# Fewer and larger parts of a down projection, its last weights kept, and a fixed place for some sums

## The chip, the cores and the metric

The kernel runs on one core of a Trainium2 chip. The metric is the device time of one execution in microseconds (us). TensorE (PE) multiplies matrices, VectorE (DVE) and ScalarE (ACT) work on rows of data, GpSimd (POOL) helps in a few places, and the queue of SyncE (SP) issues nearly all transfers between the on-chip memory and DRAM. TensorE accumulates into banks of PSUM; everything else lives in the on-chip memory, 128 partitions wide.

## The reference, cut to what matters

The reference is one layer of a decoder. 1024 prompt rows and 8 rows of running samples go through three branches, whose results are merged and projected; then comes a norm, a gated feed-forward block and a second norm.

```python
    h = layer_norm(ALPHA * x + merged @ w_out, ln1_g, ln1_b)
    gt, up = jnp.split(h @ w_gate_up, 2, axis=-1)
    h = layer_norm(ALPHA * h + (jax.nn.silu(gt) * up) @ w_down, ln2_g, ln2_b)
```

The model width is 1024 and the feed-forward width is 2816, that is 22 tiles of 128 features. All is float32.

## The kernel before, in words

Activations are kept with the features on the partitions and the 1032 rows (1024 + 8) as columns. A float32 product is made of three products of a shorter type: each operand is split into a high half (a cast on ScalarE, line 77) and a low half (what is left, a subtraction on VectorE, line 78), and high x high, high x low and low x high are accumulated in one PSUM bank (`mm3`, lines 116 to 118). So each weight piece that comes from DRAM costs one load, one cast and one subtraction before TensorE can use it.

The end of the kernel, where the change lies, has these stages:

- The output projection (`out_proj`) goes over four quarters of 258 columns. When a quarter's sums are complete, its norm (`quarter_norm`) is made while TensorE works on the next quarter: mean, differences, squares, variance, reciprocal root, product, gain and bias, store of h to DRAM, and the split of h into halves hh and hl. The norm of the last quarter runs beside the next stage.
- The first two feature tiles of gate and up (`plain_gate_up`) are plain products of h, quarter by quarter (tiles fg and fu, then ft and G). The fourth quarter of them needs the halves of the last quarter of h. Between the quarters, steps of `h_combos` are written: sums and differences of quarters of h (tile ht, and R in place, lines 1119 to 1127) with their splits (hth, htl).
- The other twenty feature tiles (`gate_up`) use those sums in a fast scheme with seven products instead of eight. Each finished tile G is stored to DRAM (line 1327).
- The down projection (`down`) reads the 22 tiles back in parts of 6, 6, 6 and 4 into two pools, gA and gB, in turn (tiles gl, the casts gh). A part is multiplied for each of 8 output tiles and three column chunks of 384, 390 and 258 columns, with its own piece of the weights (tiles wd), and added to the accumulators acc (line 1221). The accumulators start as h read back and scaled (lines 1210 and 1211).
- The last part goes chunk by chunk over all outputs (tiles dl, weights wdl), so that a chunk's second norm (`layer_norm`) can run beside the products of the next chunk. The weights of this part are loaded and split again in each of the three chunks. The third chunk has its own norm, `last_layer_norm`: it corrects the sums with the mean of the first two output tiles (tiles c0h, c0l, c and the matrix shift), and sums columns with the matrix ones (tile le) at the very end. Its scaled rows are stored, which ends the kernel.

In these stages the program order isn't the order of the queues: a planner places each instruction on its engine by estimated costs, as soon as what it needs is estimated to be ready, and an engine then executes its queue in that order. Two things bind it: data, and `issue_after(ins)`, which puts the instructions of a block, as far as they are on the engine of `ins`, behind `ins` in that engine's queue. The parts of a norm are written with it behind the last matmul of a product (`norm_step`). Pools lie on a left and a right stack of the on-chip memory; with `reuse_waits="tile"` a new tile waits for the old tiles that overlap it and not for the whole old pool. gA and gB lie on the right, where the halves of h (pool tq) and their sums (pool tx) were.

Of the kernel before, what the change touches and what calls it, by code (L numbers as in the profile page):

```python
# [10 lines left out]
F32 = mybir.dt.float32  # L11
# [7 lines left out]
P = 128  # L19
# [8 lines left out]
NM = 256  # L28
NF = 22
DEC_AT = (1, 2, 4)  # L30
FPARTS = ((0, 6), (6, 6), (12, 6), (18, 4))
PLAIN = 2
GS = 1040
NORM_AT = (0, 3)
# [25 lines left out]
class Builder:  # L60
# [14 lines left out]
    def split(self, hi, lo, src):  # L75

        ins = self.nc.scalar.copy(hi, src).ins  # L77
        self.nc.vector.tensor_sub(lo, src, hi.bitcast(F32))  # L78
        return ins

    def behind(self, ins, other):
# [886 lines left out]
    def last_layer_norm(self, n, r, product, gcol, emit):  # L968


        nc, ph = self.nc, self.ph
        ones = self.ones.bitcast(F32)
        tile_ = lambda tag, name, bufs, dt=F32: ph.tile([P, WIDE], dt, tag=tag, name=name, bufs=bufs)[:, :n]
        s1, s2 = tile_("s1", "ls1", 1), tile_("s2", "ls2", 1)
        hi, lo = (ph.tile([P, n], F32R, tag=f"c0{e}", name=f"c0{e}", bufs=1) for e in "hl")
        e1, e2 = self.bank("t", "le1")[:, :n], self.bank("t", "le2")[:, :n]

        def account(m):
            sq = s2 if m == 0 else tile_("sq", f"lsq{m}", 2)
            nc.scalar.activation(sq, r[m], AF.Square)  # L980
            if m == 7:
                return sq
            if m == 1:
                nc.vector.tensor_add(s1, r[0], r[1])
            elif m:
                nc.vector.tensor_add(s1, s1, r[m])
            if m:
                nc.gpsimd.tensor_add(s2, s2, sq)

        for m in range(KT):  # L990
            ps = product(m, last=m < LATE)
            if m in NORM_AT:
                self.norm_step()
            if m >= LATE:
                nc.tensor.matmul(ps, self.shift, hi, start=False, stop=False)
                nc.tensor.matmul(ps, self.shift, lo, start=False, stop=True)
            nc.vector.scalar_tensor_tensor(r[m], ps, 0.5, r[m], op0=ALU.mult, op1=ALU.add)
            if m == 1:
                s = tile_("xres", "lc0", 3)
                nc.vector.tensor_add(s, r[0], r[1])  # L1000
                self.split(hi, lo, s)
            elif m == LATE - 1:
                with self.tc.issue_after(self.last_mm):
                    c0 = self.bank("o", "c0")[:, :n]
                    nc.tensor.matmul(c0, self.shift, hi, start=True, stop=False)
                    nc.tensor.matmul(c0, self.shift, lo, start=False, stop=True)
                for k in range(LATE):
                    nc.vector.scalar_tensor_tensor(r[k], c0, 0.5, r[k], op0=ALU.mult, op1=ALU.add)
                    account(k)
            elif m >= LATE:  # L1010
                sq = account(m)
        nc.tensor.matmul(e1, ones, s1, start=True, stop=False)
        nc.tensor.matmul(e2, ones, s2, start=True, stop=False)
        nc.tensor.matmul(e1, ones, r[7], start=False, stop=True)
        nc.tensor.matmul(e2, ones, sq, start=False, stop=True)
        mu, rs = tile_("xres", "lmu", 3), tile_("gt", "lrs", 3)
        nc.scalar.activation(rs, e1, AF.Square)
        nc.scalar.copy(mu, e1)
        nc.vector.tensor_sub(rs, e2, rs)
        nc.scalar.activation(rs, rs, AF.Sqrt, bias=self.vec[:, V_EPS:V_EPS + 1])  # L1020
        for m in range(KT):
            (nc.vector if m < 3 else nc.gpsimd).tensor_sub(r[m], r[m], mu)
        nc.vector.reciprocal(rs, rs)
        self.norm_step()
# [8 lines left out]
    def quarter_norm(self, q, s1, h):  # L1033

        nc, r, vec = self.nc, self.R, self.vec
        cast = lambda a: a.unsqueeze(1).to_broadcast([P, 4, QN])
        yield
        mu = self.col_mean(s1, QN, f"n1mu{q}")
        sq = []
        for kh in range(2):  # L1040
            nc.vector.tensor_sub(r[q, kh], r[q, kh], cast(mu))
            sq.append(self.tq.tile([P, 4, QN], F32, tag=f"q{q}{kh}", name=f"sq{q}{kh}", bufs=2))
            nc.scalar.activation(sq[kh], r[q, kh], AF.Square)
        nc.vector.tensor_add(sq[0], sq[0], sq[1])
        nc.vector.tensor_add(sq[0][:, 0:2, :], sq[0][:, 0:2, :], sq[0][:, 2:4, :])
        nc.vector.tensor_add(sq[0][:, 0, :], sq[0][:, 0, :], sq[0][:, 1, :])
        yield
        var = self.col_mean(sq[0][:, 0, :], QN, f"n1va{q}")
        rs = self.ph.tile([P, QN], F32, tag="rs", name=f"n1rs{q}", bufs=1)
        nc.scalar.activation(rs, var, AF.Sqrt, bias=vec[:, V_EPS:V_EPS + 1])  # L1050
        nc.vector.reciprocal(rs, rs)
        for kh in range(2):
            nc.vector.tensor_mul(r[q, kh], r[q, kh], cast(rs))
            h[q, kh] = self.quarter_pair(q, kh, "h")
            for k in range(4):
                m = 4 * kh + k
                v = r[q, kh][:, k, :]
                nc.scalar.activation(v, v, AF.Identity, bias=vec[:, V_B1 + m:V_B1 + m + 1],
                                     scale=vec[:, V_G1 + m:V_G1 + m + 1])
            nc.sync.dma_start(self.scr["h"][:, 4 * kh:4 * kh + 4, q * QN:(q + 1) * QN], r[q, kh])  # L1060
            self.split(*h[q, kh], r[q, kh])

    def out_proj(self, merged):
        nc, io, ph = self.nc, self.io, self.ph
# [66 lines left out]
    def plain_gate_up(self, f, h, steps):  # L1131

        nc, io = self.nc, self.io
        wg = self.weights(io["wgu"][f], D, f"wfg{f}")
        wu = self.weights(io["wgu"][NF + f], D, f"wfu{f}")
        out = self.zt(f"G{f}")
        for q in range(4):
            x = [tuple(a[:, k % 4, :] for a in h[q, k // 4]) for k in range(KT)]
            pg = self.bank(("s", "t")[q % 2], f"fg{f}_{q}")[:, :QN]
            self.mm3(pg, list(zip(wg, x)))  # L1140
            self.norm_step()
            t = self.ph.tile([P, QN], F32, tag="gt", name=f"ft{f}_{q}", bufs=3)
            nc.scalar.activation(t, pg, AF.Tanh, scale=0.5)
            nc.vector.scalar_tensor_tensor(t, t, 1.0, pg, op0=ALU.add, op1=ALU.mult)
            pu = self.bank("mm", f"fu{f}_{q}")[:, :QN]
            self.mm3(pu, list(zip(wu, x)))
            nc.vector.tensor_mul(out[:, q * QN:(q + 1) * QN], t, pu)
            if f or q:
                next(steps, None)
        nc.sync.dma_start(self.scr["f"][:, f, :], out)  # L1150

    def plain(self, h):
# [34 lines left out]
        for _ in copies:  # L1187
            pass

    def down(self, pools):  # L1190

        nc, io, ph = self.nc, self.io, self.ph

        def load(part):
            f0, nf = FPARTS[part]
            out = []
            for j in range(nf):
                hi, lo = (pools[part % 2].tile([P, GS], F32R, tag=f"g{e}", name=f"g{e}{f0 + j}", bufs=6) for e in "hl")
                nc.sync.dma_start(lo[:, :T].bitcast(F32), self.scr["f"][:, f0 + j, :])
                out.append([(hi[:, t0:t0 + n], lo[:, t0:t0 + n]) for t0, n in CH])  # L1200
            for c in range(3):
# [2 lines left out]
                    self.split(hi, lo, lo.bitcast(F32))  # L1204
            return out

        acc = [self.zt(f"acc{m}") for m in range(KT)]
        gs = [load(0)]
        for m in range(KT):
            nc.sync.dma_start(acc[m], self.scr["h"][:, m, :])  # L1210
            nc.scalar.mul(acc[m], acc[m], ALPHA)
        for part in range(3):
            f0, nf = FPARTS[part]
            gs.append(load(part + 1))
            g = gs[part]
# [6 lines left out]
        self.norm = None  # L1222
        f0, nf = FPARTS[3]
        for c, (t0, n) in enumerate(CH):
            rs = [acc[m][:, t0:t0 + n] for m in range(KT)]

            def product(m, last=True, c=c, n=n):
                w = self.weights(io["wdn"][m][:, f0 * P:(f0 + nf) * P], nf * P, f"wdl{m}_{c}")
                ps = self.bank(("mm", "s")[m % 2], f"dl{m}_{c}")[:, :n]
                self.mm3(ps, [(w[k], gs[3][k][c]) for k in range(nf)], last)  # L1230
                return ps

            def emit(m, v, scale=1.0, t0=t0, n=n):
# [18 lines left out]
    def build(self):  # L1252
# [15 lines left out]
        with ExitStack() as right:  # L1268
# [26 lines left out]
            with pool("zf") as self.z:  # L1295
# [10 lines left out]
                with pool("gA", "right") as ga, pool("gB", "right") as gb, pool("ph5") as self.ph:  # L1306
                    self.lw = WIDE
                    self.down((ga, gb))


class FinishGate:
# [163 lines left out]
```

## Time and profile before

| what | value |
|---|---|
| median of 3 runs | 1996.84 us (1995.01 to 1997.18) |
| the profiled execution's own time | 1994.09 us |
| its span, first to last instruction | 1992.3 us |
| mean granted TensorE clock | 0.989 |
| TensorE busy | 97% |
| VectorE, ScalarE, GpSimd busy | 68%, 49%, 5% |
| fast feature tiles, 1292 to 1694 us | TensorE 402.0 of 402 us busy |
| down products up to the last part, 1694 to 1905 us | TensorE 207.6 of 211 us busy |
| last part up to the closing sums, 1905 to 1976 us | TensorE 55.6 of 71 us busy |
| from there to the end, 1976 to 1992.3 us | TensorE 2.9 of 16.3 us busy |

Times in the profile count from the first instruction. A line of the timeline has the start, the duration, the engine with its source line and operation, the tile written and the tiles read, and in brackets how long the engine stood idle before and what ended it. A line of the waits has who waited for whom, the sum in us, how often, and the longest. Matmuls overlap in the records, so the pace is taken from how many start in a stretch. An "x8" means that many instructions merged into a line.

### The profile page before, as it was taken

How to read it: one execution, taken by the hardware profiler on the slowest of the kernel's cores; microseconds unless marked ns; L12 is line 12 of the kernel's file. 1: busy time of each engine (PE TensorE's matmuls, PEld its weight loads, DVE VectorE, ACT ScalarE, POOL GpSimd, SP SyncE). 2: the span in 40 equal slices, each digit the busy share in tenths (PEclk: the TensorE clock that was granted, in tenths of full speed). 3: DMA queues.
4: the chain of work that ended last, by engine and by line, in shares of the span. 5: the costliest groups of instructions: out<-in, count | busy, mean ns of one | idle time of the engine just before them, and what ended most of it. 6: DMA issues, size and time to landing. Idle time of an engine off the chain costs nothing.

```text
span 1992.3 us, 37520 instructions
## 1 busy us (share of the span) xinstructions
PE 1934.4 (97%) x14524; PEld 1899.4 (95%) x14524; DVE 1350.9 (68%) x2746; ACT 982.8 (49%) x2099; POOL 96.7 (5%) x152
## 2 busy tenths in 40 slices
PE   9999999999999999999999999999999999999994
PEld 9999999999999998988899999899999999999994
DVE  7878987886866565498777567766565655543378
ACT  6555565464666445397764254434333333522134
POOL 1000010010000000021210000000000000000001
PEclk9999999999999999999999999999999999999997
DMA  8554545455323377667334251232222222632122
GB/s 316 168 164 160 175 163 187 136 190 172 135 91 120 124 260 236 167 190 211 109 101 157 75 199 44 71 102 92 93 87 100 86 86 80 247 112 90 58 80 101
DMA packets 155699, 275.67 MB, mean 138 GB/s; under 512 B 18992, under 2 KB 73344, under 8 KB 155520
## 3 DMA queue, kind: packets, MB, share of 16 engines
q1 hardware_dynamic: 154752, 271.17, 42.0%
q8 instruction: 114, 1.87, 0.4%
q0 software_dynamic: 768, 2.10, 0.3%
q14 instruction: 65, 0.53, 0.1%
HBM read 204.19 MB, written 73.18 MB: 139 GB/s over the span
## 4 chain that ended last, share of the span: by engine, by line
PE 82%; DMA 6%; DVE 5%; ACT 5%; issue 2%; SPq 0%; ACTq 0%; DVEq 0%; POOL 0%; POOLq 0%
PE ub L243 5%; PE ub L241 5%; PE ub L242 5%; PE ubf L241 4%; PE ubf L242 4%; PE ubf L243 4%; PE d L116 3%; PE d L117 3%; PE d L118 3%; PE ud L243 2%; PE ud L242 2%; PE ud L241 2%; PE udf L241 2%; PE udf L242 2%; PE udf L243 2%
## 5 line engine op out<-in xcount | busy, mean ns | idle before, releaser
L116 PE MATMUL d<-gh,wd_h 128*128 128x258 f32 (+2 forms) x432 | 138.3, 322 | 3.1 <-ACT gh L77 2.1
L117 PE MATMUL d<-gl,wd_h 128*128 128x390 f32 (+2 forms) x432 | 138.9, 322 | 0.2 <-DVE gl L78 0.2
L118 PE MATMUL d<-gh,wd_l 128*128 128x390 f32 (+2 forms) x432 | 138.6, 322 | 0.0
L1221 DVE SCALAR_TENSOR_TENSOR acc<-d,acc 128x384 f32<-128x384 f32 (+2 forms) x72 | 36.9, 515 | 94.3 <-PE d L118 91.5
L116 PEld LDWEIGHTS d<-gh,wd_h 128*128 128x128 f32 x432 | 81.4, 189 | 4.4 <-ACT gh L77 3.0
L117 PEld LDWEIGHTS d<-gl,wd_h 128*128 128x128 f32 x432 | 81.7, 189 | 0.5 <-DVE gl L78 0.4
L118 PEld LDWEIGHTS d<-gh,wd_l 128*128 128x128 f32 x432 | 82.0, 190 | 0.0
L118 PE MATMUL op<-mh,wol 128*128 128x258 f32 x256 | 72.3, 282 | 1.3 <-DVE wol L78 1.3
L116 PE MATMUL op<-mh,woh 128*128 128x258 f32 x256 | 72.5, 283 | 0.0
L117 PE MATMUL op<-ml,woh 128*128 128x258 f32 x256 | 72.1, 282 | 0.0
L241 PE MATMUL ub<-th,u_4h 128*128 128x258 f32 x240 | 68.6, 286 | 3.3 <-ACT u2s L266 3.3
L594 ACT ACTIVATE bp<-bp,bst 128x257 f32<-128x257 f32 (+1 forms) x128 | 62.8, 493 | 17.3 <-DVE bst L590 17.0
L241 PE MATMUL ub<-th,u_0h 128*128 128x258 f32 x240 | 68.3, 284 | 1.1 <-ACT zb L1346 1.1
L243 PE MATMUL ub<-th,u_4l 128*128 128x258 f32 x240 | 68.9, 287 | 0.0
L242 PE MATMUL ub<-tl,u_4h 128*128 128x258 f32 x240 | 68.4, 285 | 0.0
L241 PE MATMUL ub<-th,u_2h 128*128 128x258 f32 x240 | 68.0, 283 | 0.3 <-ACT p1s L266 0.3
L243 PE MATMUL uc<-th,u_3l 128*128 128x258 f32 x240 | 68.2, 284 | 0.0
L243 PE MATMUL ub<-th,u_2l 128*128 128x258 f32 x240 | 68.2, 284 | 0.0
L243 PE MATMUL ud<-th,u_1l 128*128 128x258 f32 x240 | 68.2, 284 | 0.0
L243 PE MATMUL ub<-th,u_0l 128*128 128x258 f32 x240 | 68.2, 284 | 0.0
L243 PE MATMUL ub<-th,u_6l 128*128 128x258 f32 x240 | 68.2, 284 | 0.0
L243 PE MATMUL ud<-th,u_5l 128*128 128x258 f32 x240 | 68.1, 284 | 0.0
(880 smaller groups left out, 7879.0 us busy)
## 6 DMA issues: line engine op xcount, KB each, us to landing
ur<-win SPq DMA_DIRECT2D x120, 256.0 KB, 2.9
urf<-wgu SPq DMA_DIRECT2D x80, 256.0 KB, 2.7
scr_f<-G SPq DMA_DIRECT2D x22, 516.0 KB, 2.8
gl<-scr_f SPq DMA_DIRECT2D x22, 516.0 KB, 5.9
dck<-cmk SPq DMA_DIRECT2D x32, 256.0 KB, 3.0
dcv<-cmvT SPq DMA_DIRECT2D x32, 256.0 KB, 3.5
st<-scr_q SPq DMA_DIRECT2D x32, 256.0 KB, 4.6
scr_g<-za SPq DMA_DIRECT2D x12, 516.0 KB, 3.4
```

The costliest lines, as they stand in the source:

```text
L116: nc.tensor.matmul(ps, sh, mh, start=opens and i == 0, stop=False)
L117: nc.tensor.matmul(ps, sh, ml, start=False, stop=False)
L118: self.last_mm = nc.tensor.matmul(ps, sl, mh, start=False, stop=closes and i == last).ins
L241: mm(sh[:, w], xh, start=opens and k == 0, stop=False)
L242: mm(sh[:, w], xl, start=False, stop=False)
L243: self.last_mm = mm(sl[:, w], xh, start=False, stop=k == 3).ins
L594: nc.scalar.activation(x, x, AF.Exp, bias=st[:, g:g + 1], scale=-1.0, accum_out=st[:, 4 + g:5 + g])
L1221: nc.vector.scalar_tensor_tensor(a, ps, 0.5, a, op0=ALU.mult, op1=ALU.add)
```

## The change

The down projection has three parts of 8, 7 and 7 feature tiles. The first and third use pool gA (8 buffers of each half), the second gB (7). Only two parts are accumulated over all outputs; the third is the last part. After the second part pool gB is closed and a pool wl takes its place; it holds the split weights of the last part for all eight outputs (16 tiles of 896 columns), which are loaded and split in the first chunk, in pieces of 512 and 384 columns, and used again in the second and third. Three small tiles of the last norm get fewer buffers. In `plain_gate_up`, the steps of `h_combos` are put behind `norm_end`, the last subtraction of the last quarter's norm, in VectorE's queue.

```diff
-FPARTS = ((0, 6), (6, 6), (12, 6), (18, 4))
+FPARTS = ((0, 8), (8, 7), (15, 7))
...
         ins = self.nc.scalar.copy(hi, src).ins
-        self.nc.vector.tensor_sub(lo, src, hi.bitcast(F32))
+        self.last_lo = self.nc.vector.tensor_sub(lo, src, hi.bitcast(F32)).ins
         return ins
...
-                s = tile_("xres", "lc0", 3)
+                s = tile_("xres", "lc0", 2)
...
-        mu, rs = tile_("xres", "lmu", 3), tile_("gt", "lrs", 3)
+        mu, rs = tile_("xres", "lmu", 2), tile_("gt", "lrs", 1)
...
             self.split(*h[q, kh], r[q, kh])
+        self.norm_end = self.last_lo
...
             if f or q:
-                next(steps, None)
+                with self.tc.issue_after(self.norm_end):
+                    next(steps, None)
...
-    def down(self, pools):
+    def down(self, ga, pool):
...
-        def load(part):
+        def load(part, pool):
             f0, nf = FPARTS[part]
-            out = []
+            out, bufs = [], FPARTS[part % 2][1]
             for j in range(nf):
-                hi, lo = (pools[part % 2].tile([P, GS], F32R, tag=f"g{e}", name=f"g{e}{f0 + j}", bufs=6) for e in "hl")
+                hi, lo = (pool.tile([P, GS], F32R, tag=f"g{e}", name=f"g{e}{f0 + j}", bufs=bufs) for e in "hl")
...
+        acc = [self.zt(f"acc{m}") for m in range(KT)]
+        with pool("gB", "right") as gb:
+            g0 = load(0, ga)
+            for m in range(KT):
+                nc.sync.dma_start(acc[m], self.scr["h"][:, m, :])
+                nc.scalar.mul(acc[m], acc[m], ALPHA)
+            g1 = load(1, gb)
+            product(0, g0)
+            g2 = load(2, ga)
+            product(1, g1)
+        with pool("wl", "right") as wl:
+            self.last_products(acc, g2, wl)
+
+    def last_products(self, acc, g, pool):
+        nc, io, ph = self.nc, self.io, self.ph
+        self.norm, w = None, []
+        f0, nf = FPARTS[2]
         for c, (t0, n) in enumerate(CH):
             rs = [acc[m][:, t0:t0 + n] for m in range(KT)]

             def product(m, last=True, c=c, n=n):
-                w = self.weights(io["wdn"][m][:, f0 * P:(f0 + nf) * P], nf * P, f"wdl{m}_{c}")
+                if c == 0:
+                    hi, lo = (pool.tile([P, nf * P], F32R, tag="wl", name=f"wl{e}{m}", bufs=16) for e in "hl")
+                    for a, b in ((0, 512), (512, nf * P)):
+                        raw = self.half_raw(io["wdn"][m][:, f0 * P + a:f0 * P + b], b - a, f"wl{m}r{a}")
+                        self.split(hi[:, a:b], lo[:, a:b], raw[:, :b - a])
+                    w.append([(hi[:, k * P:(k + 1) * P], lo[:, k * P:(k + 1) * P]) for k in range(nf)])
                 ps = self.bank(("mm", "s")[m % 2], f"dl{m}_{c}")[:, :n]
-                self.mm3(ps, [(w[k], gs[3][k][c]) for k in range(nf)], last)
+                self.mm3(ps, [(w[m][k], g[k][c]) for k in range(nf)], last)
                 return ps
```

More of the change, by code (lines that the diff above doesn't have):

```diff
@@ L1205, in load, with product @@
             return out
[L1207 to L1212, printed above, removed]
+        def product(part, g):
             f0, nf = FPARTS[part]
-            gs.append(load(part + 1))
-            g = gs[part]
             for m in range(KT):
@@ L1221, in down @@
                     nc.vector.scalar_tensor_tensor(a, ps, 0.5, a, op0=ALU.mult, op1=ALU.add)
-        self.norm = None
-        f0, nf = FPARTS[3]
+        acc = [self.zt(f"acc{m}") for m in range(KT)]
[14 more added lines that the diff above has]
+        f0, nf = FPARTS[2]
         for c, (t0, n) in enumerate(CH):
@@ L1305, in build @@
                 right.close()
-                with pool("gA", "right") as ga, pool("gB", "right") as gb, pool("ph5") as self.ph:
+                with pool("gA", "right") as ga, pool("ph5") as self.ph:
                     self.lw = WIDE
-                    self.down((ga, gb))
+                    self.down(ga, pool)
 class FinishGate:
```

## The prediction

> **What bounds the kernel now.** I read the sums of the page first, then busy time by stage, then TensorE's waits, then VectorE's order of work where those waits fall.
>
> ```profile
> PE 1934.4 (97%) x14524; PEld 1899.4 (95%) x14524; DVE 1350.9 (68%) x2746; ACT 982.8 (49%) x2099; POOL 96.7 (5%) x152
> ...
> 1300.00:1400.00 100.00, 100.00 (x834) 100.00 (x833) 60.27 (x95) 38.88 (x79) 0.00 (x0) 1.00 0.28 94
> 1800.00:1900.00 100.00, 100.00 (x637) 100.00 (x636) 35.22 (x72) 17.50 (x36) 0.00 (x0) 1.00 0.24 73
> ...
> 1253.00:1268.00 15.00, 10.66 (x64) 9.65 (x63) 10.80 (x13) 9.05 (x15) 0.00 (x0) 0.77 0.32 105
> ...
> 1905.00:1976.00 71.00, 55.56 (x310) 52.77 (x309) 62.00 (x118) 32.07 (x61) 5.04 (x6) 0.90 0.28 82
> 1976.00:1992.30 16.30, 2.85 (x8) 1.76 (x8) 10.72 (x21) 9.53 (x20) 3.63 (x5) 0.52 0.46 163
> ```
>
> TensorE is the bound nearly everywhere, so a change that keeps the number of matmuls can only win where TensorE stands or runs at a lower clock. The full pace is 100/834 = 0.120 us for a matmul of 258 columns and, over the mix of 384, 390 and 258 columns in the down products, 100/637 = 0.157 us, or 0.47 us for one set of three. (In these rows the second field of each engine is its count; the field after POOL is the granted clock.)
>
> Two stretches fall short. Between 1253 and 1268 us only 64 matmuls ran: 64 x 0.120 = 7.7 us of work in 15, so 7.3 us are lost, at a granted clock of 0.77. The last quarter of the output projection's norm falls there. Between 1905 and 1976 us the last part of the down products runs: 4 tiles x 8 outputs x 3 terms = 96 sets at 0.47 = 45.1 us, and some 2.7 us of small matmuls for the norms (eighteen, which I put at 0.15 each by the paces above), so 47.8 of 71 us: 23.2 us are lost.
>
> ```profile
> PE dl L118 <- DVE wdl_l L78: 8.4, 3, 5.3
> PE le L1012 <- DVE ls L986: 2.6, 1, 2.6
> PE fg L116 <- DVE ft L1144: 2.5, 1, 2.5
> PE d L116 <- ACT gh L77: 2.1, 2, 1.3
> PE fg L116 <- ACT hh L77: 1.4, 1, 1.4
> ...
> 1941.32 4.31 DVE L955 SCALAR_TENSOR_TENSOR acc<-acc,vec,n2rs 128x384 f32<-128x384 f32 x8
> 1946.50 0.68 DVE L78 TENSOR_TENSOR wdl_l<-wdl_1r__24009,wdl_h 128x512 fp32r<-128x512 f32 x1
> ...
> 1942.00:1946.00 4.00, 0.00 (x0) 0.00 (x0) 4.00 (x8) 4.00 (x8) 0.00 (x0) 1.00 0.65 234
> 1946.00:1950.00 4.00, 2.77 (x8) 2.77 (x9) 3.46 (x7) 0.28 (x1) 0.00 (x0) 0.51 0.81 235
> ```
>
> The longest wait of the tail is for the low half of reloaded weights (8.4 us). The split of one piece takes 0.68 us, but in VectorE's queue it stands behind eight scalings of the norm of chunk 0 (4.31 us): TensorE does nothing from 1942 to 1946 and then runs at a clock of 0.51.
>
> **The change part by part.** First, the sums of h. Now the sums and splits for the fast units stand between the links of the last quarter's norm:
>
> ```profile
> 1242.10 1.23 DVE L1119 TENSOR_TENSOR ht<-R,R 128x1032 f32<-128x1032 f32 x1
> 1243.25 1.22 DVE L1044 TENSOR_TENSOR sq<-sq,sq 128x1032 f32<-128x1032 f32 x1
> 1244.39 1.23 DVE L1122 TENSOR_TENSOR R<-R,R 128x1032 f32<-128x1032 f32 x1
> 1245.53 0.69 DVE L1045 TENSOR_TENSOR sq<-sq 128x516 f32<-128x516 f32 x1
> ...
> 1249.77 1.22 DVE L78 TENSOR_TENSOR htl<-R,hth 128x1032 fp32r<-128x1032 f32 x1
> 1250.92 1.76 DVE L1051 RECIPROCAL n1rs<-n1rs 128x258 f32<-128x258 f32 x1
> 1252.59 1.17 DVE L89 SCALAR_TENSOR_TENSOR htl<-R,hth 128x1032 fp32r<-128x1032 f32 x1
> 1253.68 2.36 DVE L1053 TENSOR_TENSOR R<-R,n1rs 128x1032 f32<-128x1032 f32 x2
> ...
> 1258.48 1.23 DVE L78 TENSOR_TENSOR hl<-R,hh 128x1032 fp32r<-128x1032 f32 x1 [0.63 <-ACT hh L77]
> ...
> 1262.06 1.23 DVE L78 TENSOR_TENSOR hl<-R,hh 128x1032 fp32r<-128x1032 f32 x1
> 1263.21 0.68 DVE L78 TENSOR_TENSOR wfg_l<-wfg1r__16461,wfg_h 128x512 fp32r<-128x512 f32 x1
> ...
> 1248.97 0.48 ACT L1050 ACTIVATE n1rs<-n1va3p,vec 128x258 f32<-128x258 f32 x1 [0.28 <-PE n1va3p L930]
> ```
>
> L1122 delays L1045 by 1.14 us, two more keep the reciprocal back from 1249.45, where the square root ended, to 1250.92 (1.47), and L89 delays L1053 by 1.09: 3.7 us for certain. L1119 ahead of L1044, and a split ahead of the variance's low half, add up to 1.15 us each. I take 5 of 3.7 to 6.0. The halves hl then come at 1253.5 and 1257.1 instead of 1258.5 and 1262.1 and are done 1.2 us later. TensorE, out of work at about 1253.5, waits some 1.2 us for the first, has 24 matmuls (2.9 us) on it, and some 0.7 us for the second: 1.9 us. What is late next: the moved operations, eight of about 1.15 us for the first half of the columns, now start together at about 1258, and beside them stand four splits of the second feature tile's weights (0.68 us each), needed from about 1261. If all four go behind all eight, TensorE waits until 1258.3 + 9.2 + 0.7 = 1268, 7 us; if they slip between, nothing. The fast units themselves want the sums only near 1290. I take 1.4 us, since the splits depend on nothing but a free buffer and each moved operation depends on one before it: 7.3 - 1.9 - 1.4 = **4.0 us won** (between 5.4 won and 1.6 lost).
>
> A clock of 0.77 over these 15 us is 3.4 us of clock, so 2 to 3 of the 7.3 us come from the clock and not from waiting. I take it as whole once the waits are short; if it is halved all the same, 4.0 becomes about 2. [...]
>
> Second, the drains. Three parts instead of four take 24 accumulations off VectorE; they lie beside a busy TensorE (VectorE 35% between 1800 and 1900, TensorE 100%). Won: 0. Without that cover nothing would be lost, since the work only shrinks.
>
> Third, the opening of the down products. Part 0 grows from 6 to 8 feature tiles:
>
> ```profile
> gl<-scr_f SPq DMA_DIRECT2D x22, 516.0 KB, 5.9
> ...
> 1689.64 2.16 SPq L1199 DMA_DIRECT2D gl<-scr_f  x4
> 1696.35 0.32 SPq L1327 DMA_DIRECT2D scr_f<-G  x1
> 1696.72 1.32 SPq L1199 DMA_DIRECT2D gl<-scr_f  x2
> 1698.09 5.09 SPq L1210 DMA_DIRECT2D acc<-scr_h  x8
> ...
> 1704.00:1712.00 8.00, 6.30 (x35) 5.82 (x36) 4.97 (x11) 7.48 (x13) 0.00 (x0) 1.00 1.03 416
> ```
>
> The queue of SP has four loads, then waits for the last gate product's store, then two loads. The DMA engines are full (share 1.03, 416 GB/s), so a load of 516 KB (0.53 MB) costs 1.27 us, two more 2.5 us, and the loads of acc behind them are that much later. The two tiles that now come after the store give TensorE 2 x 3 x 0.47 = 2.8 us of work on the first output, which covers the 2.5 if four loads still go ahead of the store. If all eight go behind it, the last lands about 4 x 1.27 + 2.5 = 7.6 us later than now's last. I take **1 us lost**, between 1 won and 6 lost (7.6, less part of that cover).
>
> Fourth, the kept weights go into the space of part 1's feature tiles. Each product of part 1 reads them all, so the first kept piece can be written only while the last group of 21 matmuls (2.5 us) runs. Cast and split (0.62 and 0.68 us for 512 columns) fit under it if they wait tile by tile; if they wait for the whole space, TensorE stands about 1.5 us. I take **0.5 us lost**, between 0 and 1.5. Afterwards an output has 1.1 + 1.2 us of casts and splits beside 21 matmuls of 384 columns, some 3.6 us: covered.
>
> Fifth, the tail. Chunks 1 and 2 no longer reload: 16 loads, 16 casts and 16 splits (16 x 0.68 = 10.9 us of VectorE) fall away there, and with 7 tiles instead of 4 the matmuls over the same norms grow by 7/4. The last part is now 168 sets, 79.0 us, with the 2.7 us of small ones. VectorE's work in chunk 2, beside 168 x 0.120 = 20.2 us and about 2 us of small matmuls:
>
> ```profile
> L946 DVE TENSOR_TENSOR n2s<-n2s,n2sq 128x384 f32<-128x384 f32 (+1 forms) x14 | 7.8, 556 | 0.1
> L953 DVE RECIPROCAL n2rs<-n2rs 128x384 f32<-128x384 f32 (+1 forms) x2 | 5.1, 2562 | 0.0
> L942 DVE TENSOR_TENSOR acc<-acc,n2mu1p 128x390 f32<-128x390 f32 x8 | 4.2, 556 | 0.0
> L997 DVE SCALAR_TENSOR_TENSOR acc<-dl,acc 128x258 f32<-128x258 f32 x8 | 3.3, 420 | 0.7 <-PE dl L118 0.5 <-PE dl L996 0.2
> ...
> 1968.36 5.44 POOL L988 TENSOR_TENSOR ls<-ls,lsq 128x258 f32<-128x258 f32 x6 [937.91 <-ACT lsq L980]
> 1970.29 1.22 DVE L78 TENSOR_TENSOR wdl_l<-wdl_2r__24265,wdl_h 128x512 fp32r<-128x512 f32 x1
> ```
>
> Half of L946 (3.9), L942 (4.2), L997 (3.3), four splits of sums (2), twelve corrections and sums of 0.4 (5) make 18.4 us; the reciprocal (2.6) and eight scalings (4.3) come to 25.3. The first 18.4 fit under 22; the rest may be put after the last product, as half of the scalings is now. The variance of chunk 1, 12 us of chained work after its mean, is ready at about 13 of those 22 us, the shift's correction at 15, GpSimd's six additions (5.4) at about 21.5, so that almost nothing is left to wait for. Remaining waits: 1.0 for the variance and the correction, whose places in TensorE's order are fixed beforehand, 1.5 for a reciprocal (2.6) put among the last sums, 0.3 for the two means: 2.8. So 23.2 - 2.8 = **20.4 us won** (22.5 if two thirds of the waits vanish, 12 if VectorE, slowed beside GpSimd as the split of 1.22 us was, becomes the bound). After the last product I take 0: up to 2 us may be won if more scalings come before it.
>
> Sum: 4.0 - 1 - 0.5 + 20.4 = 22.9 us. The profiled execution took 1994.09 us (span 1992.3), so it would be 1971.2; the median of the runs shown lies 2.75 above it, which I keep: 1996.84 - 22.9 = **1973.9**.
>
> **Rivals.** (a) The sums' wait passes to the weights of the second feature tile: 1.6 lost instead of 4.0 won, 1979.5. For it: both queue on VectorE at 1258; against it: the present order is mixed one by one. (b) The opening waits: all eight loads behind the store, 6 instead of 1 lost, 1978.9. For it: two already are. (c) The tail becomes VectorE's: 12 instead of 20.4 won, 1982.3. For it: 62 of 71 us busy now; against it: 10.9 us leave. (d) Slower: part 0's eight loads go behind the store and share the DMA engines evenly with the eight of acc and the seven of part 1, since the queue waits for none of them. 23 x 1.27 = 29 us after 1696.7 plus 4 us to land: part 0 complete at 1730 instead of 1703, 27 us lost instead of 1, 1999.9. It outweighs the rest once part 0 is complete later than about 1727. Against it: the queue issues in order and the first loads land first now. (e) The change does not do what it says in the tail: the kept pieces are written so late that chunk 0 stalls for each; that needs over 3.6 us of casts and splits for an output, and there are 2.3.
>
> **How the numbers follow.** The forecast 0.58; (a) 0.12; (b) 0.13; (c) 0.10; (d) 0.03; (e), or a mix that leaves nothing (1996.8), 0.04. The forecast's own bounds reach from 1967 (5.4 and 22.5 won, 2 after the last product, nothing lost) to 1978; (a), (b), (c) and two of them together carry the upper end to 1984. A measurement of this kernel tells about 0.2% (4 us) from no change: faster 0.93 (the forecast and a to c), same 0.04 (e), slower 0.03 (d).
>
> **What would show it.** Right: no wait for wdl_l; TensorE between the first kept product and the final sums (le) over 95% busy at a clock near 1; hl of the last quarter near 1254 and 1258; the last part starting near 1868 (1905.1 now, less three tiles, 72 sets, 33.8 us, less 4.0, plus 1). Wrong: TensorE waiting for wfg_l or wfu_l after 1258, gl loads landing past 1710, L986 or L997 late at the end, or the norm's links still apart by 1.14 us.

## The result and the profile after

The changed kernel took 1974.55 us (median, 1972.81 to 1975.36), the kernel before 1997.01 us beside it: a ratio of 0.9888 with a 95% interval of 0.9871 to 0.9905, 22.5 us less. The forecast was 1973.9, 22.9 us less.

The profiled execution of the changed kernel took 1975.36 us, with a span of 1973.6. First the sums of its page and busy time by stage. In the rows of a stage the fields are the stretch in us from the span's start, its length and TensorE's busy time with its count of matmuls, then weight loads, VectorE, ScalarE and GpSimd, then the granted clock, the share of the DMA engines and GB/s. The stages are cut where the first matmul of a tile starts: op (output projection), fg (first two feature tiles and the last quarter's norm), ubf (the twenty fast tiles), d (parts before the last), dl (last part), le (closing sums).

```profile
PE 1928.8 (98%) x14524; PEld 1896.1 (96%) x14524; DVE 1331.1 (67%) x2698; ACT 971.7 (49%) x2075; POOL 96.5 (5%) x152
...
1144.80:1240.50 95.70, 94.02 (x783) 93.61 (x782) 71.88 (x117) 49.66 (x75) 0.00 (x0) 1.00 0.38 133
1240.50:1289.30 48.80, 47.52 (x390) 46.79 (x390) 39.14 (x50) 26.88 (x38) 0.00 (x0) 1.00 0.17 55
1289.30:1697.20 407.90, 404.27 (x3362) 403.93 (x3360) 246.02 (x386) 162.78 (x328) 0.00 (x0) 1.00 0.29 95
1697.20:1874.50 177.30, 175.03 (x1081) 173.65 (x1081) 69.66 (x143) 47.73 (x100) 0.00 (x0) 0.97 0.35 123
1874.50:1958.00 83.50, 82.64 (x523) 81.91 (x523) 59.49 (x111) 28.32 (x55) 4.94 (x6) 1.00 0.14 47
1958.00:1973.60 15.60, 2.46 (x8) 1.27 (x8) 10.99 (x21) 9.08 (x19) 3.59 (x5) 0.65 0.48 170
```

The same cut of the kernel before:

```profile
1139.80:1235.60 95.80, 94.09 (x783) 93.62 (x782) 71.81 (x117) 49.69 (x75) 0.00 (x0) 1.00 0.38 133
1235.60:1290.00 54.40, 50.06 (x391) 48.85 (x390) 39.85 (x50) 26.97 (x38) 0.00 (x0) 0.94 0.15 49
1290.00:1695.50 405.50, 404.19 (x3362) 403.94 (x3360) 244.25 (x384) 160.35 (x326) 0.00 (x0) 1.00 0.28 93
1695.50:1905.10 209.60, 207.55 (x1296) 206.29 (x1297) 88.61 (x185) 57.09 (x120) 0.00 (x0) 0.99 0.35 119
1905.10:1975.90 70.80, 55.36 (x309) 52.57 (x307) 61.80 (x118) 31.89 (x60) 5.04 (x6) 0.90 0.28 82
1975.90:1992.30 16.40, 2.95 (x8) 1.86 (x8) 10.82 (x21) 9.63 (x20) 3.63 (x5) 0.53 0.46 162
```

Three feature tiles, 72 sets of three matmuls (33.8 us at 0.47), moved from the parts before the last into the last part. With the stages' lengths taken to a hundredth from the matmuls' starts, and those 33.8 us moved over in the row of before:

| stage | before | after | difference |
|---|---|---|---|
| output projection (op to fg) | 95.75 | 95.61 | -0.1 |
| first two feature tiles (fg to ubf) | 54.41 | 48.82 | -5.6 |
| fast tiles and the wait behind them (ubf to d) | 405.54 | 407.94 | +2.4 |
| parts before the last (d to dl) | 209.59 - 33.8 = 175.8 | 177.24 | +1.4 |
| last part (dl to le) | 70.78 + 33.8 = 104.6 | 83.55 | -21.0 |
| closing sums to the end | 16.42 | 15.59 | -0.8 |
| sum | 852.5 | 828.8 | -23.7 |

The two spans differ by 18.7 and not by 23.7 us because this execution of the changed kernel started its output projection at 1144.8 us, 5.0 us later than the one of before (1139.8), with the same TensorE instructions in the same order up to there. That is scatter: a second execution of the changed kernel (below) started it at 1139.5. So stages are compared here, and medians, but not the spans of two single executions.

Now TensorE's waits in the stages concerned (who waited for whom, the sum in us, how often, the longest):

```profile
PE d L116 <- ACT gh L77: 5.2, 2, 3.6
...
PE fg L116 <- ACT hh L77: 0.8, 1, 0.8
PE le L1012 <- DVE ls L986: 0.8, 1, 0.8
...
PE dl L116 <- ACT wlh L77: 0.7, 1, 0.7
...
PE fg L117 <- DVE hl L78: 0.5, 1, 0.5
```

The wait for wdl_l (8.4 us) is gone, that of le for ls went from 2.6 to 0.8, that of fg for ft (2.5) is gone, and the wait of the opening for gh grew from 2.1 to 5.2, while two smaller ones there (1.0 for acc, 0.2 for gl) went. VectorE's order in the norm of the last quarter is now this:

```profile
1247.26 1.23 DVE L1044 TENSOR_TENSOR sq<-sq,sq 128x1032 f32<-128x1032 f32 x1 [0.19 <-ACT sq L1043]
1248.53 0.69 DVE L1045 TENSOR_TENSOR sq<-sq 128x516 f32<-128x516 f32 x1
...
1253.21 1.76 DVE L1051 RECIPROCAL n1rs<-n1rs 128x258 f32<-128x258 f32 x1
1255.00 2.38 DVE L1053 TENSOR_TENSOR R<-R,n1rs 128x1032 f32<-128x1032 f32 x2
...
1259.83 1.23 DVE L78 TENSOR_TENSOR hl<-R,hh 128x1032 fp32r<-128x1032 f32 x1 [0.77 <-ACT hh L77]
1262.40 1.23 DVE L78 TENSOR_TENSOR hl<-R,hh 128x1032 fp32r<-128x1032 f32 x1 [1.35 <-ACT hh L77]
1263.56 1.23 DVE L1120 TENSOR_TENSOR ht<-R,R 128x1032 f32<-128x1032 f32 x1
1264.70 0.68 DVE L78 TENSOR_TENSOR wfg_l<-wfg1r__16461,wfg_h 128x512 fp32r<-128x512 f32 x1
1265.30 1.23 DVE L1123 TENSOR_TENSOR R<-R,R 128x1032 f32<-128x1032 f32 x1
...
1272.83 0.68 DVE L78 TENSOR_TENSOR wfg_l<-wfg1r__16467,wfg_h 128x512 fp32r<-128x512 f32 x1
1273.44 0.68 DVE L78 TENSOR_TENSOR wfu_l<-wfu1r__16473,wfu_h 128x512 fp32r<-128x512 f32 x1
```

The links of the norm follow each other without a sum between them. Counted from the stage's start, the splits of hl start at 19.3 and 21.9 us (1240.5 here) where they started at 22.9 and 26.5 (1235.6 before). Behind hl the weights' splits slip in between the sums.

### The profile page after: what moved, and what is told of

Same layout as the page of the kernel before. It is cut to its first block, busy times and chain, and to the rows that moved or that the text cites. A ratio compares the mean times of both kernels' runs of the same rounds, so it can differ in the third digit from the quotient of the medians.

```text
span 1973.6 us, 37334 instructions
## 1 busy us (share of the span) xinstructions
PE 1928.8 (98%) x14524; PEld 1896.1 (96%) x14524; DVE 1331.1 (67%) x2698; ACT 971.7 (49%) x2075; POOL 96.5 (5%) x152
## 4 chain that ended last, share of the span: by engine, by line
PE 86%; DMA 5%; ACT 5%; DVE 3%; issue 1%; SPq 0%; ACTq 0%; POOL 0%; DVEq 0%; POOLq 0%
PE ub L243 5%; PE ub L241 5%; PE ub L242 5%; PE ubf L241 4%; PE ubf L242 4%; PE ubf L243 4%; PE d L116 3%; PE d L117 3%; PE d L118 3%; PE ud L243 3%; PE ud L242 3%; PE ud L241 3%; PE udf L241 2%; PE udf L242 2%; PE udf L243 2%; PE brs L116 2%
## 5 line engine op out<-in xcount | busy, mean ns | idle before, releaser
L116 PE MATMUL d<-gh,wd_h 128*128 128x384 f32 (+2 forms) x360 | 116.4, 326 | 5.2 <-ACT gh L77 5.2
L117 PE MATMUL d<-gl,wd_h 128*128 128x384 f32 (+2 forms) x360 | 116.7, 324 | 0.0
L118 PE MATMUL d<-gh,wd_l 128*128 128x384 f32 (+2 forms) x360 | 116.0, 323 | 0.0
L1216 DVE SCALAR_TENSOR_TENSOR acc<-d,acc 128x384 f32<-128x384 f32 (+2 forms) x48 | 24.6, 515 | 91.5 <-PE d L118 91.5
L116 PEld LDWEIGHTS d<-gh,wd_h 128*128 128x128 f32 x360 | 68.5, 191 | 6.3 <-ACT gh L77 5.7
L117 PEld LDWEIGHTS d<-gl,wd_h 128*128 128x128 f32 x360 | 68.8, 191 | 0.3 <-DVE gl L78 0.3
L118 PEld LDWEIGHTS d<-gh,wd_l 128*128 128x128 f32 x360 | 68.9, 192 | 0.0
L241 PE MATMUL ub<-th,u_6h 128*128 128x258 f32 x240 | 68.1, 284 | 0.0
```

The lines of the kernel that those rows point to most:

```text
L116: nc.tensor.matmul(ps, sh, mh, start=opens and i == 0, stop=False)
L117: nc.tensor.matmul(ps, sh, ml, start=False, stop=False)
L118: self.last_mm = nc.tensor.matmul(ps, sl, mh, start=False, stop=closes and i == last).ins
L241: mm(sh[:, w], xh, start=opens and k == 0, stop=False)
```

## The experiments

**Each half of the change alone.** The first kernel is the one before with nothing but the place of the sums changed; the second is the changed kernel without it.

```diff
# e1: in the kernel before (and norm_end kept from quarter_norm)
-                next(steps, None)
+                with self.tc.issue_after(self.norm_end):
+                    next(steps, None)
# e2: in the changed kernel
-                with self.tc.issue_after(self.norm_end):
-                    next(steps, None)
+                next(steps, None)
```

> Only the sums of h are put behind the last quarter's norm; parts of 6, 6, 6 and 4, weights of the last part reloaded. Theory (the order on VectorE held the norm back): the 7.3 us lost by TensorE in the 15 us after the third quarter fall to about 2, nothing else moves: 997 to 1 split of the gain, about 5.5 us faster than before (1991.5). Rival (the wait passes on to the split weights of the second feature tile): 0 to 2 us slower than before, with TensorE waiting for wfg_l or wfu_l.

> The down projection as in the changed kernel, the sums of h free as before. Theory (the two edits add up): 5.5 us slower than the changed kernel, 1980, and the stall of about 7 us beside the last quarter's norm is back. Rival (the two share a cause, such as the run's own drift): within 2 us of the changed kernel.

The sums alone: 1991.13 us, ratio 0.9967 (0.9955 to 0.9979), with 48.83 us from fg to ubf and all later stages as before (405.60, 209.57, 71.07). The parts alone: 1979.42 us, 0.9905 (0.9879 to 0.9930), with 54.61 us in that stage. The two add up: 1 - 0.9967 and 1 - 0.9905 make 0.0128, the whole change 0.0112, within their intervals. So the sums are worth about 6 us and the parts about 18, and neither lives off the other.

**Could the wait have passed to the second feature tile's weights?** That was rival (a). Here the four splits of these weights are held behind the last sum of the first half in VectorE's queue, which is what the planner could have done by itself; the casts, on ScalarE, stay where they were.

```diff
-        wg = self.weights(io["wgu"][f], D, f"wfg{f}")
-        wu = self.weights(io["wgu"][NF + f], D, f"wfu{f}")
+        with self.tc.issue_after(self.last_lo) if f else nullcontext():
+            wg = self.weights(io["wgu"][f], D, f"wfg{f}")
+            wu = self.weights(io["wgu"][NF + f], D, f"wfu{f}")
```

> The changed kernel, with the splits of the second plain feature tile's weights put behind all eight sums and splits of the first half of the columns in VectorE's queue: the case that the prediction feared, made on purpose. Theory: TensorE waits some 5 to 7 us for wfg_l, with a halved clock after it 6 to 9 us lost, 1981 to 1983. Rival (there is slack in that order): under 2 us lost.

1985.42 us, 0.9941 (0.9921 to 0.9961): 57.87 us from fg to ubf instead of 48.82, longer than before the change. TensorE's waits of this kernel from 1255 to 1300 us, and its busy time while VectorE works through the sums:

```profile
PE fg L118 <- DVE wfg_l L78: 3.6, 1, 3.6
PE fu L116 <- DVE G L1149: 2.1, 1, 2.1
PE fg L116 <- DVE ft L1146: 1.4, 1, 1.4
```

```profile
1272.00:1280.00 8.00, 2.62 (x12) 2.41 (x13) 6.52 (x9) 1.05 (x1) 0.00 (x0) 0.65 0.30 105
```

7.1 us of waits that the changed kernel doesn't have, and a clock of 0.65 beside them. The wait for wfg_l itself is shorter than the 5 to 7 us that I expected, the stage's loss of 9.1 us is at the upper end of 6 to 9, and the median lies above the 1981 to 1983. So the rival was real and dearer than its price: it would have made this edit 3.5 us slower than before (57.87 against 54.41). That it didn't come about rests on where the planner put the four splits.

**The last part: kept weights or more work to hide behind?** In e3 the parts stay 6, 6, 6 and 4, but the last part's weights are kept for seven of the eight outputs (there was no room for all); the eighth reloads. In e4 the parts are 8, 7 and 7, but the weights are loaded and split again in each chunk.

```diff
# e3: FPARTS of before; in the last part
-                w = self.weights(io["wdn"][m][:, f0 * P:(f0 + nf) * P], nf * P, f"wdl{m}_{c}")
+                if m == KT - 1:
+                    w = self.weights(io["wdn"][m][:, f0 * P:(f0 + nf) * P], nf * P, f"wdl{m}_{c}")
+                else:
+                    if c == 0:
...
+                        kept.append([(hi[:, k * P:(k + 1) * P], lo[:, k * P:(k + 1) * P]) for k in range(nf)])
+                    w = kept[m]
# e4: in the changed kernel
-                if c == 0:
...
-                    w.append([(hi[:, k * P:(k + 1) * P], lo[:, k * P:(k + 1) * P]) for k in range(nf)])
+                w = self.weights(io["wdn"][m][:, f0 * P:(f0 + nf) * P], nf * P, f"wdl{m}_{c}")
```

> Sums as in the changed kernel; parts of 6, 6, 6 and 4 as before, but the split weights of the last part are kept for seven of the eight outputs (the eighth is still reloaded in each chunk, for want of space). Theory (VectorE is too busy for the short products, the reloads being only a part): the stretch from the first product of the last part to the closing sums falls from 71 to about 64 us, so some 7 us (5 to 10) faster than with the sums alone, about 1984.5. Rival (the reloads alone make the waits): the stretch falls to 55 us or less, 15 us or more faster than with the sums alone, 1976 or less.

> Sums and parts of 8, 7 and 7 as in the changed kernel, but the weights of the last part are loaded and split again in each of the three chunks. Theory (longer products are cover, reloads are load): the last stretch is 92 to 99 us instead of 83.6 in the changed kernel, so 8 to 15 us slower than that, 1983 to 1990. Rival (reloads alone matter): the stretch is about 104, no better than before for its work, 1995. Other rival (cover alone matters): within 2 us of the changed kernel.

Keeping alone: 1982.19 us, 0.9919 (0.9899 to 0.9938), and 64.48 us in the last part against 70.78, 6.3 won. More work alone: 1985.34 us, 0.9935 (0.9915 to 0.9955), and 97.29 against 104.6, 7.3 won. Both lengths are about as expected (64, and 92 to 99). Both edits together: 21.0 won, more than the 13.6 of the two. TensorE's waits in the last part say why. With kept weights and four tiles:

```profile
PE le L1012 <- DVE ls L986: 10.0, 1, 10.0
PE dl L996 <- DVE c0l L78: 2.4, 1, 2.4
```

With seven tiles and reloaded weights:

```profile
PE dl L118 <- DVE wdl_l L78: 7.1, 4, 2.4
PE dl L116 <- DVE acc L997: 2.1, 1, 2.1
```

In e3 no wait for weights is left, but the norms of chunks 1 and 2 are too long for the products beside them, and TensorE waits 10.0 us at the very end for VectorE's sums. In e4 there are products enough, but each piece must be split again by the same VectorE. Each edit alone leaves TensorE waiting for VectorE. In e3 VectorE works from 1939.6 to 1966.9 us, where the wait for ls ends, with one break over 0.2 us (1.1); in e4 it is busy for 77.66 of the 97.3 us, and the splits that TensorE waits for stand in its queue behind the norms. The last row of the changed kernel's last part shows how near it still is:

```profile
1935.00:1958.00 23.00, 22.25 (x184) 21.84 (x182) 20.94 (x41) 9.52 (x20) 4.94 (x6) 1.00 0.01 1
```

In the last 23 us VectorE works 20.94 and TensorE 22.25.

**The opening.** The queue of SP in the changed kernel (start, duration, issuing line, tile written and read; of an "x7" the duration is that of the seven issues together):

```profile
1689.29 0.90 SPq L1222 DMA_DIRECT2D acc<-scr_h  x2
1690.29 0.38 SPq L1201 DMA_DIRECT2D gl<-scr_f  x1
1695.73 0.32 SPq L1343 DMA_DIRECT2D scr_f<-G  x1
1696.10 4.49 SPq L1201 DMA_DIRECT2D gl<-scr_f  x7
1700.64 6.88 SPq L1222 DMA_DIRECT2D acc<-scr_h  x6
```

One load of part 0 goes ahead of the last gate product's store, and seven behind it, where it was four and two. The first trial was to swap the sizes, and then to give part 0's loads a queue of their own.

```diff
# e5 and e10
-FPARTS = ((0, 8), (8, 7), (15, 7))
+FPARTS = ((0, 7), (7, 8), (15, 7))
# e7: that, and
-                nc.sync.dma_start(lo[:, :T].bitcast(F32), self.scr["f"][:, f0 + j, :])
+                (nc.gpsimd if part == 0 else nc.sync).dma_start(lo[:, :T].bitcast(F32), self.scr["f"][:, f0 + j, :])
```

> The changed kernel with parts of 7, 8 and 7: pool gA (14 buffers) then overlaps only the halves of h and not their sums. Theory (in the changed kernel all but one of part 0's loads stand behind the last gate product's store, because the pool reaches into the tiles that the last fast unit reads): four loads go ahead of the store again, TensorE loses about 7 us instead of 10 around 1693 to 1720, and the kernel is 3 us faster than the changed one, about 1971.5. Rival (part 0 is late because the DMA engines are full, whatever the order): within 1 us of the changed kernel.

> Parts of 7, 8 and 7, and part 0's loads issued from GpSimd's queue, which is empty there, so that none stands behind the store. Theory (the order in SP's queue makes the opening's loss): TensorE loses 4 us or less around 1693 to 1720 instead of 10, 5 to 6 us faster than the changed kernel, 1969. Rival (the DMA engines are the limit, or descriptors written by GpSimd come slower): no better than parts of 7, 8 and 7 alone, or worse.

Parts of 7, 8 and 7: 1970.77 us, 0.9863 (0.9844 to 0.9882), with 405.61 us from ubf to d and 174.43 from d to dl (407.94 and 177.24 with 8, 7 and 7), 5.1 us better where I expected 3. The queue has four loads ahead of the store again:

```profile
1688.59 1.85 SPq L1201 DMA_DIRECT2D gl<-scr_f  x4
1695.17 0.32 SPq L1343 DMA_DIRECT2D scr_f<-G  x1
1695.59 1.74 SPq L1201 DMA_DIRECT2D gl<-scr_f  x3
```

With part 0's loads in GpSimd's queue: 1970.32 us, 0.9859 (0.9843 to 0.9876), 173.57 us from d to dl, but 0.4 us more at the end. In time that is no difference to e5 that these runs can tell, and the gain over e5 that I expected (1969 against 1971.5) didn't come. The waits of the opening did fall, to 1.3 us for gh and 0.4 for gl (2.3, 1.1 for acc and 0.2 in e5), but the granted clock of its first 21 us was 0.92 instead of 1.00. That the engines of the transfers keep it from being worth more is likely and not shown: they are at a share of 1.03 right after the opening, as before the change.

```profile
1706.00:1714.00 8.00, 7.80 (x47) 7.46 (x47) 4.55 (x10) 8.00 (x14) 0.00 (x0) 1.00 1.03 416
```

Swapping the sizes changes two things: part 0 has fewer tiles, and pool gA is smaller. By the layout of the on-chip memory, gA with 16 buffers of 1040 columns (66,560 bytes in each partition) reaches 512 bytes into the last tile of the sums' low halves, which the fast products still read (the halves of h, in whose place the pool lies, are 16 tiles of 4,128 bytes, 66,048); a load into that place waits for the last of them, and the planner moves others ahead of it. Only 1032 of the 1040 columns are used, so 16 buffers of 1032 end short of that tile. They make pool gB smaller, too, but gB had 16 buffers of 1040 columns in e5, where four loads went ahead. That tells the two apart with part 0 left at eight tiles:

```diff
-                hi, lo = (pool.tile([P, GS], F32R, tag=f"g{e}", name=f"g{e}{f0 + j}", bufs=bufs) for e in "hl")
+                hi, lo = (pool.tile([P, T], F32R, tag=f"g{e}", name=f"g{e}{f0 + j}", bufs=bufs) for e in "hl")
```

> The changed kernel with tiles of 1032 instead of 1040 columns in the pools gA and gB (only 1032 are used). Theory: what the opening of the down products lost comes from the size of gA, 16 buffers of 4160 bytes, which reach 512 bytes into the last tile of the sums of h that the fast products still read; with 4128 bytes they end short of it, so that four of part 0's loads go ahead of the last gate product's store again, as before the change, and four behind it. The fast tiles with the wait after them then take 405.6 us instead of 407.9, and the parts before the last 175 to 176 instead of 177.2: 3 to 4 us better than the changed kernel, a median of about 1971. Rival: eight tiles are too many for the opening wherever they lie, since the engines of the transfers are full: 407 to 408 and 177 again, no change from 1974.5.

> The kernel with parts of 7, 8 and 7 tiles once more, beside the changed kernel on one chip. By its stages (405.6 and 174.4 us against 407.9 and 177.2) it is 5 us better than the changed kernel, whose median was 1974.6: about 1969.5. If the stages of the profiled runs were an accident, the two differ by less than 2 us.

> The changed kernel itself, for a comparison on one chip: 1974.5, ratio 0.989 to the kernel before, with 407.9 and 177.2 us in the two stages; where its output projection starts may differ by some us, as it did among the kernels so far (1139.8 to 1146.1 us after the first instruction).

On one chip: the changed kernel again 1973.32 us, 0.9882 (0.9864 to 0.9899); narrow tiles 1968.50 us, 0.9859 (0.9839 to 0.9878); parts of 7, 8 and 7 again 1972.78 us, 0.9877 (0.9857 to 0.9896). The stages from ubf to d and from d to dl are 407.55 and 177.53 in the changed kernel, 405.63 and 174.49 with narrow tiles, 405.61 and 176.08 with 7, 8 and 7. With narrow tiles the queue is this, with eight tiles in part 0:

```profile
1684.33 1.85 SPq L1201 DMA_DIRECT2D gl<-scr_f  x4
1690.77 0.32 SPq L1343 DMA_DIRECT2D scr_f<-G  x1
1691.14 2.25 SPq L1201 DMA_DIRECT2D gl<-scr_f  x4
```

So the theory holds: with eight tiles in part 0, four loads go ahead again, and the changed kernel loses 5.0 us in these stages (3 to 4 expected; 4.8 by the medians) to 512 bytes, not to the eighth tile. The size is less sure than the cause: one profiled execution of each kernel stands behind the stages, and the clock alone can make 1.7 us of it, as the rows below show. All four runs of narrow tiles (1965.96 to 1971.14) lie below all four of the changed kernel (1971.30 to 1974.62). The kernel with narrow tiles has the lowest median of the study, though its interval overlaps with both others'. That the second run of 7, 8 and 7 stood level with the changed kernel missed my expectation of 5 us. Two things are in its profiled execution: it started the output projection at 1145.2 us where the changed kernel's started at 1139.5, scatter as above, and the clock. Its other three runs (1970.76 to 1973.07) have no profile; for them the cause stays open, and the times don't settle what the swap of sizes alone is worth. These are the first 21 us from d, in turn of the changed kernel again, of narrow tiles, of 7, 8 and 7 at first and of 7, 8 and 7 again:

```profile
1692.90:1713.90 21.00, 19.07 (x91) 17.91 (x92) 13.18 (x29) 13.96 (x29) 0.00 (x0) 0.77 1.01 391
```

```profile
1689.90:1710.90 21.00, 18.15 (x103) 16.84 (x104) 14.46 (x31) 16.97 (x32) 0.00 (x0) 1.00 1.00 389
```

```profile
1694.30:1715.30 21.00, 18.69 (x104) 17.40 (x105) 12.97 (x28) 15.73 (x29) 0.00 (x0) 1.00 1.00 388
```

```profile
1696.30:1717.30 21.00, 18.68 (x96) 17.43 (x97) 12.99 (x28) 15.40 (x29) 0.00 (x0) 0.92 1.00 389
```

The last two are one kernel with the same waits in the opening (2.3 us for gh, 1.1 for acc, 0.2 for gl in both), and yet the granted clock is 1.00 in one and 0.92 in the other. That is 0.08 x 21 = 1.7 us, the difference between 174.43 and 176.08. In the changed kernel the granted clock is short by 0.23 x 21 = 4.8 us. Its waits are only about 1 us longer (5.2 against 2.7 for gh, 1.3 for acc and 0.2 for gl with narrow tiles), so of the 5.0 us that its opening loses against narrow tiles about 4 are left for the clock.

**The hand-over to the kept weights.** Here the new pool waits for all of part 1's pool instead of tile by tile.

```diff
-        with pool("wl", "right") as wl:
+        with self.tc.tile_pool(name="wl", bufs=1, side="right", reuse_waits="pool") as wl:
```

> The changed kernel, with the pool of kept weights waiting for the whole of part 1's pool instead of tile by tile. Theory: the wait before the first kept product grows from 0.9 to about 2 us, and nothing else changes: 1 us, hardly to be seen in the time, but in the wait of dl for wlh. Rival (the first kept product waits for something else): the same 0.9 us.

1971.51 us, 0.9871 (0.9851 to 0.9891), and the wait at the first kept product is the same 0.7 us:

```profile
PE dl L116 <- ACT wlh L77: 0.7, 1, 0.7
```

The expected growth to 2 us didn't come. Each product of part 1 reads all its tiles, which would explain it: the first tile then comes free hardly earlier than the whole pool.

## Why the prediction was right, and where it wasn't

**The tail** (20.4 won) was the main term, and it stands: 21.0. The last part was to take 79.0 + 2.7 + 2.8 = 84.5 us and took 83.55, at a clock of 1.00. The remaining waits are 0.7 for the first kept piece and 1.1 at the end (for ls and acc), not the 2.8 that I put on the variance, the correction and a reciprocal among the sums. Rival (c), VectorE as the bound, was nearer than its chance of 0.10 says: 20.94 of 23 us, and e3 and e4 show it deciding as soon as half of the edit is missing. Rival (e) falls with the wait of 0.7.

**The sums of h** (4.0 won) were mis-sized: 5.6. Of its three parts, the 7.3 lost before (54.4 us less 390 matmuls at 0.120 are 7.6) and the 1.9 that remain (48.8 less 46.8 are 2.0) held, the second partly by luck: I had put the splits of hl 5 us earlier, 17.9 and 21.5 us after the stage's start, and they started 3.6 and 4.6 earlier, at 19.3 and 21.9. The links won the 3.7 that I had called certain and not the rest, but TensorE ran out of work later as well (18.6 us after the start instead of 17.9), so that its waits came out as forecast. The third, 1.4 for the second feature tile's weights, measured 0: between 1263.56 and 1276 the splits stand among the sums, and no wait for wfg_l or wfu_l is left. The choice to count the clock as whole once the waits are short was an estimate of mine with no run behind it; in this stage it came true: 1.00, against 0.94 before, and 0.06 x 54.4 = 3.3 us of the 5.6 can be the clock's. As a value between "slip between" and "all behind" the 1.4 was too cautious for the order that came, and rival (a), 1.6 lost, too mild for the one that didn't: e6 puts it at 3.5 lost.

**The opening** (1 lost) was mis-sized the other way. Fast tiles and parts before the last lost 3.8 together; without the 0.7 at the hand-over, 3.1. The step that failed is "if four loads still go ahead of the store": one did. I had looked at the loads and the DMA engines, and not at where a pool of 16 buffers ends. The bound of 6 held it, and the mechanism is close to rival (b), seven loads behind the store instead of eight. With narrow tiles the condition is met, and the two stages take 405.63 + 174.49 = 580.1 us against 405.54 + 175.8 = 581.3 before: nothing lost, as the bound of 1 won had it, though the clock was 1.00 there and 0.92 before. I had also priced the loss as lateness of transfers alone. Against the kernel before the opening's waits are 1.9 us longer (5.2 against 3.3), which leaves 1.2 of the 3.1 to the clock (0.77 against 0.92).

**The hand-over** (0.5 lost) is a wait of 0.7; **the closing** (0) won 0.8, within its bound of 2, and I didn't follow it further; **the drains** (0) have no run of their own: between e1, with the old parts, and the kernel with narrow tiles the parts before the last differ by 209.57 - 33.8 - 174.49 = 1.3 us, and one step of the clock (0.92 against 1.00) is 1.7. Rival (d) didn't show: no wait for part 0 was over 3.6 us.

So the sum of 22.9 against 23.7 by stages and 22.5 by medians is in part a meeting of errors: 1.6 too little for the sums, 0.6 too little in the last part, 0.8 too little at the close, against 2.3 too little lost at the opening and the hand-over. The dates I gave (last part near 1868) came 6 us later, 5 of it by the scatter ahead of the output projection.

## What to carry to other kernels

When work stands at the end of a busy engine's chain, making the chain shorter and giving the other engine more to do beside it can each be worth little (6.3 and 7.3 us here) and together three times as much (21.0): look for which engine is still the bound after the first edit. When a pool grows, see what lies at its new end: 512 bytes over a tile that is still read put seven of eight loads behind a store here, where without them it was four. And an edit that moves work behind a point should be checked for what else queues there; here it went well only because the splits found places in between.

## What the runs showed of the hardware

The granted clock in the first 21 us from d took four values in eleven of the profiled executions: 1.00 (e5 and narrow tiles), 0.92 (the kernel before, e1, e7 and e10), 0.84 (e4 and e8) and 0.76 to 0.77 (e2 and both executions of the changed kernel). They lie about 0.08 apart, that is 1.7 us of clock at a time. The row of the kernel before, and shorter rows of the same stretch:

```profile
1695.50:1716.50 21.00, 18.95 (x99) 17.69 (x100) 12.12 (x26) 13.17 (x25) 0.00 (x0) 0.92 0.99 386
...
1696.00:1698.00 2.00, 1.77 (x6) 1.45 (x7) 2.00 (x5) 2.00 (x6) 0.00 (x0) 0.72 0.75 297
1698.00:1700.00 2.00, 2.00 (x8) 2.00 (x7) 2.00 (x6) 1.60 (x5) 0.00 (x0) 0.50 1.01 295
1700.00:1702.00 2.00, 2.00 (x14) 2.00 (x13) 1.46 (x4) 0.00 (x0) 0.00 (x0) 0.93 1.01 353
```

The missing 0.28, 0.50 and 0.07 of 2 us each are the 1.7 us, in one piece of 3.4 us at a clock of 0.50, from 1696.9 to 1700.3. Ahead of it lie a wait of 1.3 us, which ended at 1695.5, and one of 0.2; the other two waits of this opening (0.8 and 1.0 us) ended at 1704.7 and 1709.0, and the clock stayed whole there (1.00 from 1702 to 1716). With the same waits it was 1.00 once and 0.92 once in the kernel with parts of 7, 8 and 7. With a first wait of 3.3 to 3.6 us it was 0.77 in both executions of the changed kernel, but 0.84 in e4 and e8 (3.4 and 3.5 us), so the length of the wait alone doesn't set it.

My estimate that the clock is whole once the waits are short doesn't hold in the opening of the kernel before: the longest wait there was 1.3 us, and 1.7 us of clock were lost all the same. What sets off such a piece, and when, these runs don't show.

The other surprise was the scatter ahead of the change. Among the thirteen profiled executions, whose TensorE instructions are the same in the same order up to the output projection, its start lay between 1139.4 and 1146.1 us, and for the changed kernel alone at 1144.8 and 1139.5. Between two of them part of it goes with the clock. In the first execution of the changed kernel, which started it at 1144.8 us, the granted clock was 0.50 for 3.4 us in two places, from 703.2 to 706.6 and from 771.5 to 774.9 us (0.83 over 700 to 710 us, 0.76 over 769 to 776); in the kernel before, which started it at 1139.8, it was 1.00 over both stretches. Each such piece is 1.7 us of clock, and the two can make 3.4 of the 5.0 us between these two executions. What leads to it, and what makes the rest of the scatter, stays open. The scatter is as large as the opening's whole loss, so single executions of this kernel can't be compared by their spans below about 7 us. Stages can be compared more closely, but not all alike: the first two feature tiles took 48.80 to 48.85 us in all ten kernels and repeats that move the sums and nothing else there, while the output projection, the same in all thirteen, took 95.0 to 98.8.
